# Low-rank forget gates as one 48-row float32r product, and block-diagonal state reads in four 32-column tiles

## The chip, the cores and the metric

The kernel runs on one core of a Trainium2 chip. The metric is the device time of one execution in microseconds (us). Five engines share the work: PE (matmul, with its weight loads shown apart as PEld), DVE (elementwise and reductions), ACT (activations and copies), POOL (elementwise, memset) and SP, whose queue issues every DMA of this kernel.

## What is computed

One layer of a hybrid trunk runs over 2048 prompt tokens, 16 meta tokens and 8 samples of 16 tokens each (D_MODEL 1024). All its inputs are one projection of the normalised rows `h`. Two parts of the gated linear attention (GLA, 4 heads, keys of 128, values of 256) matter here:

```python
log_f = log_sigmoid(g_low @ gla_w2 + gla_gate_b) / GLA_TAU      # g_low: [t, 16], gla_w2: [16, 512]
# per token: S_t = diag(exp(log_f_t)) S_{t-1} + k_t^T v_t ; o_t = q_t S_t
o = einsum('bhid,bhde->bhie', qc * exp(b), s) + einsum('bhij,bhje->bhie', a, vc)
```

The prompt starts from a zero state. Each of the 8 samples starts from a state of its own, `state_gla[b, h]` (128 x 256), so the term `(q exp b) s` takes another `s` for every 16 of the 128 sample rows. The second branch (an indexer that selects 256 keys per query, then attention over them) is not touched.

## The kernel before

`phase1` normalises and transposes the rows, projects them with all columns of the weights, and writes the results to DRAM scratch. `phase_keys` opens it: it goes through the 18 row tiles (meta, 16 of the prompt, the samples), makes the transposed `h` of each (`prep_x`) and the columns needed first (`keys`): attention keys and values, the indexer's key and the 16 gate columns `g_low`. `keys` is a generator in two parts, and the second part of one tile is issued after the first part of the next (`KLAG = 1`). In its second part it transposes the indexer's key and `g_low` into one PSUM tile `ps`, splits the key into high and low halves (`kih` on ACT, `kil` on DVE), copies the 16 gate rows to a small tile `gl` on ACT (L353) and stores them to the scratch `d["gl"]` [16, 2192] by SP (L354). The small tiles of `keys` (`xi`, `xd`, `gl`) share four buffers, tag `evs`. Three projection groups follow (`project`), and in their shadow DVE runs the selection. Projections are written as three float32r products each (`mm3`, L264 to L266): high x high, high x low, low x high.

`phase2` runs attention (`attend`) as the main stream, and beside it a list of side work: `gla_gates`, then `attend_sample`, `gla_sample`, and the 16 prompt chunks of GLA. The first 13 items of it are issued at a priority 1500 earlier than the main stream, so `gla_gates` begins while the last group of `project` is still on PE.

`gla_gates` takes the 2192 columns in five chunks (four of 512 and one of 144). It loads `gl` [16, n] from the scratch (L658), multiplies it for each of 4 heads with `w2` [16, 512] in float32 (L666), which appears as two matmul records per product, and forms the log sigmoid from Abs, Exp and Ln on ACT, a min on DVE and a subtraction on POOL. `w2` is loaded straight from the input (L957) in `gla_pools`, when phase 2 is set up.

`gla_sample` reads the sample states. For each head it loads two tiles `s0` of four states each, clears a tile `qx` [128, 8, 128] on POOL (L923), scatters the queries of sample `b` to columns 16b to 16b+15 of `qx[:, b, :]` (DVE), and adds up eight float32 products of `qx[:, b, :]` with the state of sample `b` in one PSUM tile `po` (L928), 128 columns wide each of which 112 are zero. One product `a` x `v` follows (L929), then the update of the eight states (L935).

The program is built with an ordering pass: instructions are put in order on each engine by priority and by a simulated timeline. So the order in which an engine meets its instructions is fixed in the program, and a change of one operation can move others.

Of the kernel before, what the change touches and what calls it, by code (L numbers as in the profile page):

```python
# [10 lines left out]
F32 = mybir.dt.float32  # L11
F32R = mybir.dt.float32r
# [5 lines left out]
OP = mybir.AluOpType  # L18
# [3 lines left out]
P = 128  # L22
# [6 lines left out]
NB = 8  # L29
# [89 lines left out]
class Trunk:  # L119
# [73 lines left out]
    def scratch(self, ctx):  # L193
        dr = ctx.enter_context(self.tc.tile_pool(name="dr", bufs=1, space=DRAM))
        d = {}
        for n, s, t in (
            ("gq", [512, TT], F32), ("gk", [512, TT], F32), ("gl", [16, TT], F32), ("lf", [512, TT], F32),
            ("gv", [TT, 1024], F32), ("gr", [TT, 1024], F32),
            ("q", [2048, TT], F32R),
            ("ih", [512, TT], F32R), ("il", [512, TT], F32R),  # L200
            ("kd", [P, 4, TT], F32R), ("v", [TT, 256], F32), ("z", [TT, 1024], F32),
            ("ma", [1024, TT], F32), ("mb", [1024, TT], F32),
            ("oa", [1024, TT], F32), ("ob", [1024, TT], F32), ("ya", [1024, TT], F32), ("h", [TT, 1024], F32),
        ):
            d[n] = dr.tile(s, t, name="d_" + n)
        d["mask"] = {j: dr.tile([P, nkeys(j)], BF16, name=f"d_mask{j}") for j in range(16)}
        d["mask"]["s"] = dr.tile([P, SKEY], BF16, name="d_masks")
        d["xt"] = [dr.tile([P, KT, n], F32, name=f"d_xt{q}") for q, n in enumerate(PCN)]
        self.d = d
# [102 lines left out]
    def keys(self, t, x, c, w1, w2):  # L312
# [36 lines left out]
        nc.tensor.transpose(ps[:16, 1, :r], xi[:r, 64:80], self.ident[:r, :r])  # L349
        kc = NKEY if t == "s" else (0 if t == "m" else META + t * P)  # L350
        self.split(self.kih[:, kc : kc + r], self.kil[:, kc : kc + r], ps[:, 0, :r])
        gl = self.ev.tile([16, P], F32, name="gl", tag="evs", bufs=4)
        nc.scalar.copy(gl[:, :r], ps[:16, 1, :r])  # L353
        nc.sync.dma_start(d["gl"][:, c0 : c0 + r], gl[:, :r])  # L354

    def phase_keys(self):

# [294 lines left out]
    def gla_gates(self):  # L652

        nc = self.nc
        for c in range(0, TT, 512):
            n = min(512, TT - c)
            gl = self.gt.tile([16, 512], F32, name="gl", tag="x")
            nc.sync.dma_start(gl[:, :n], self.d["gl"][:, c : c + n])  # L658
            xs, es = [], []
            for g in range(2):  # L660
                x = self.sb.tile([P, 2, 512], F32, name="gx", tag="s4", bufs=SKB)
                e = self.sb.tile([P, 2, 512], F32, name="ge", tag="s4", bufs=SKB)
                for u in range(2):
                    h = 2 * g + u
                    ps = self.pg.tile([P, 512], F32, name="pg")
                    nc.tensor.matmul(ps[:, :n], self.w2[:, h * P : (h + 1) * P], gl[:, :n], start=True, stop=True)  # L666
                    self.act(e[:, u, :n], ps[:, :n], AF.Abs, bias=self.gb[:, h : h + 1])
                    self.ts(x[:, u, :n], ps[:, :n], self.gb[:, h : h + 1], OP.add, 0.0, OP.min)
                self.act(e[:, :, :n], e[:, :, :n], AF.Exp, scale=-1.0)
                xs.append(x)  # L670
                es.append(e)
            for g in range(2):
                x, e = xs[g][:, :, :n], es[g][:, :, :n]
                self.act(e, e, AF.Ln, bias=1.0)
                self.tt(x, x, e, OP.subtract, eng=nc.gpsimd)
                nc.sync.dma_start(self.d["lf"][2 * g * P : (2 * g + 2) * P, c : c + n].rearrange("(h p) t -> p h t", p=P), x)
            yield
# [214 lines left out]
    def gla_sample(self):  # L892
# [20 lines left out]
        for half in range(2):  # L913
            po = self.pg.tile([P, 2, 256], F32, name="pg")
            for u in range(2):
                h = 2 * half + u
                s0 = []
                for w in range(2):
                    t = self.sb.tile([P, 4, 256], F32, name="s0", tag="s4", bufs=SKB)
                    nc.sync.dma_start(t[:], self.i["state_gla"][0, 4 * w : 4 * w + 4, h].rearrange("b k v -> k b v"))  # L920
                    s0.append(t)
                qx = self.sb.tile([P, NB, P], F32, name="qx", tag="s4", bufs=SKB)
                nc.gpsimd.memset(qx[:], 0.0)  # L923
                dg = qx[:].rearrange("p b (c s) -> p (b c) s", s=NS)[:, :: NB + 1, :]
                self.tt(dg.rearrange("p (n u) (w s) -> p n u w s", u=2, w=2), qt[:, h, :, 0:4, :].rearrange("p n (u w) s -> p n u w s", w=2),
                        f[1][0][:, NB * h : NB * h + NB].rearrange("p (n u) w -> p n u w", u=2)[:, :, :, :, None].to_broadcast([P, 4, 2, 2, 8]), OP.mult)
                for bb in range(NB):
                    nc.tensor.matmul(po[:, u, :], qx[:, bb, :], s0[bb // 4][:, bb % 4, :], start=bb == 0, stop=False)  # L928
                nc.tensor.matmul(po[:, u, :], a[:, h, :], v[:, h, :], start=False, stop=True)  # L929
                for bp in range(4):  # L930
                    bs = slice(2 * bp, 2 * bp + 2)
                    vx = self.gm.tile([P, 2, 256], F32, name="vx", tag="m")
# [16 lines left out]
    def gla_pools(self, c):  # L949
# [3 lines left out]
        self.gm = c.enter_context(tc.tile_pool(name="gm", bufs=2))  # L953
        self.pg = c.enter_context(tc.tile_pool(name="pg", bufs=PGB, space=PSUM))
        gc = c.enter_context(tc.tile_pool(name="gc", bufs=1))
        self.w2 = gc.tile([16, 512], F32, name="w2")
        nc.sync.dma_start(self.w2[:], i["gla_w2"][0])  # L957
        self.gb = gc.tile([P, 4], F32, name="gb")
        nc.sync.dma_start(self.gb[:], i["gla_gate_b"][0].rearrange("(h p) -> p h", p=P))
        self.lm = gc.tile([P, 864], U8, name="lm")  # L960
        with tc.tile_pool(name="lf", bufs=1) as lf:
            t = lf.tile([P, 864], F32, name="lmf")
            nc.sync.dma_start(t[:], i["c_levels"])
            nc.vector.tensor_copy(self.lm[:], t[:])
        return gc


# [503 lines left out]
```

## Time and profile before

| | us |
|---|---|
| median of 3 runs | 3657.09 |
| lowest and highest | 3652.93, 3662.06 |
| the profiled execution, its own time | 3653.39 |
| its span, first to last instruction | 3651.6 |
| mean granted TensorE clock | 0.985 of full speed |

Busy time is the time in which an engine executes; an engine that is not busy waits for a semaphore, or has nothing to do. The columns of the windows view are busy us of each engine with the number of its instructions, then the granted clock, the DMA engines' busy share and GB/s. In the views by line, a group's row ends with the idle time of the engine ahead of the group and what ended it. A float32 matmul stands in the trace as two records, a float32r one as one. Records of PE overlap: the distance from start to start is the pace, not the duration of one.

### The profile page before, as it was taken

How to read it: one execution, taken by the hardware profiler on the slowest of the kernel's cores; microseconds unless marked ns; L12 is line 12 of the kernel's file. 1: busy time of each engine (PE TensorE's matmuls, PEld its weight loads, DVE VectorE, ACT ScalarE, POOL GpSimd, SP SyncE). 2: the span in 40 equal slices, each digit the busy share in tenths (PEclk: the TensorE clock that was granted, in tenths of full speed). 3: DMA queues.
4: the chain of work that ended last, by engine and by line, in shares of the span. 5: the costliest groups of instructions: out<-in, count | busy, mean ns of one | idle time of the engine just before them, and what ended most of it. 6: DMA issues, size and time to landing. Idle time of an engine off the chain costs nothing.

```text
span 3651.6 us, 65899 instructions
## 1 busy us (share of the span) xinstructions
PE 3516.6 (96%) x24196; PEld 3224.6 (88%) x24196; DVE 2568.0 (70%) x5971; ACT 1451.5 (40%) x3084; POOL 1048.6 (29%) x1220
## 2 busy tenths in 40 slices
PE   7999999999999999999989999999999999989999
PEld 7999999999999999998976778777778888879998
DVE  7748997799999988943246877777765666555444
ACT  4444223433334234325434555555665443431110
POOL 3122343242343344344301433334410000012221
PEclk9999999999999999999999999999999999999999
DMA  8642443263442345363653333233343345564432
GB/s 266 196 127 84 136 124 96 84 180 106 122 127 75 117 136 166 115 173 122 160 170 106 84 92 85 80 92 85 85 116 89 94 106 138 150 193 140 121 114 62
DMA packets 535810, 448.78 MB, mean 123 GB/s; under 512 B 94032, under 2 KB 507856, under 8 KB 535488
## 3 DMA queue, kind: packets, MB, share of 16 engines
q1 hardware_dynamic: 535488, 444.58, 42.4%
q8 instruction: 190, 3.11, 0.4%
q14 instruction: 132, 1.08, 0.1%
HBM read 288.01 MB, written 156.44 MB: 122 GB/s over the span
## 4 chain that ended last, share of the span: by engine, by line
PE 75%; DVE 13%; DMA 5%; ACT 2%; issue 2%; POOL 1%; SPq 1%; POOLq 0%; DVEq 0%; ACTq 0%
PE pp L266 12%; PE pp L264 12%; PE pp L265 12%; PE oo L1070 6%; PE px L1046 4%; PE pd L264 3%; PE pd L266 3%; PE pd L265 3%; PE pl L1110 2%; PE pl L1111 2%; PE fo L264 2%; PE fo L265 2%; PE fo L266 2%; DVE junk L149 1%; DVE sc L152 1%
## 5 line engine op out<-in xcount | busy, mean ns | idle before, releaser
L149 DVE TENSOR_SCALAR_CACHE_REDUCE junk<-sc,cand 128x272 bf16<-128x272 f32 (+6 forms) x512 | 701.7, 1371 | 17.0
L143 POOL TENSOR_TENSOR wlo<-raw,whi 128x512 fp32r<-128x512 f32 x360 | 487.9, 1376 | 768.0 <-ACT whi L158 704.3
L266 PE MATMUL pp<-whi,xl 128*128 128x256 f32 (+3 forms) x1952 | 560.4, 288 | 4.4 <-DVE xl L143 4.4
L264 PE MATMUL pp<-whi,xh 128*128 128x256 f32 (+3 forms) x1952 | 561.7, 288 | 3.1 <-ACT whi L158 2.1
L264 PE MATMUL pp<-xh,whi 128*128 128x384 f32 (+2 forms) x1728 | 563.0, 326 | 1.4 <-ACT whi L158 1.4
L265 PE MATMUL pp<-xl,whi 128*128 128x384 f32 (+2 forms) x1728 | 563.2, 326 | 0.0
L266 PE MATMUL pp<-xh,wlo 128*128 128x384 f32 (+2 forms) x1728 | 562.1, 326 | 0.1
L265 PE MATMUL pp<-wlo,xh 128*128 128x256 f32 (+3 forms) x1952 | 560.9, 288 | 0.0
L266 PEld LDWEIGHTS pp<-whi,xl 128*128 128x128 f32 (+1 forms) x1952 | 370.4, 190 | 14.6 <-DVE xl L143 6.9
L264 PEld LDWEIGHTS pp<-whi,xh 128*128 128x128 f32 (+1 forms) x1952 | 371.4, 190 | 11.2 <-issue 3.0
L265 PEld LDWEIGHTS pp<-wlo,xh 128*128 128x128 f32 (+1 forms) x1952 | 371.4, 190 | 5.4 <-issue 2.3
L1112 DVE CUSTOM_DVE_ANT_0 lgl<-pl,mkl 128x348 f32<-128x348 f32 (+8 forms) x608 | 297.3, 510 | 83.6 <-PE pl L1111 48.0
L1110 PE MATMUL pl<-kd,q 128*128 128x348 f32 (+14 forms) x800 | 308.1, 388 | 32.7 <-DVE mx L1112 23.9
L264 PE MATMUL pd<-xh,wh 128*128 128x242 f32 (+3 forms) x1152 | 327.9, 285 | 8.6 <-ACT wh L1328 3.8
L264 PEld LDWEIGHTS pp<-xh,whi 128*128 128x128 f32 x1728 | 324.4, 188 | 2.7 <-ACT whi L158 2.0
L266 PE MATMUL pd<-xh,wl 128*128 128x242 f32 (+3 forms) x1152 | 324.6, 282 | 0.8 <-POOL wl L143 0.8
L265 PE MATMUL pd<-xl,wh 128*128 128x242 f32 (+3 forms) x1152 | 325.1, 282 | 0.3 <-DVE xl L143 0.3
L266 PEld LDWEIGHTS pp<-xh,wlo 128*128 128x128 f32 x1728 | 324.1, 188 | 1.2 <-POOL wlo L143 0.4
L265 PEld LDWEIGHTS pp<-xl,whi 128*128 128x128 f32 x1728 | 324.4, 188 | 0.7
L158 ACT CAST whi<-raw 128x512 fp32r<-128x512 f32 (+1 forms) x344 | 199.1, 622 | 314.8 <-DMA raw<-in_w_in 201.3
L155 ACT ACTIVATE lgl<-lgl,mx 128x1040 f32<-128x1040 f32 (+7 forms) x256 | 249.8, 976 | 181.5 <-DVE mx L1114 177.6
L1118 POOL COPY pmeta<-lgl 128x48 f32<-128x48 f32 x256 | 58.7, 229 | 771.4 <-ACT lgl L155 765.0
(250 smaller groups left out, 7842.7 us busy)
## 6 DMA issues: line engine op xcount, KB each, us to landing
raw<-in_w_in SPq DMA_DIRECT2D x360, 256.0 KB, 3.2
q<-d_q SPq DMA_DIRECT2D x272, 128.0 KB, 3.0
d_h<-x SPq DMA_DIRECT2D x17, 512.0 KB, 3.4
d_gv<-en SPq DMA_DIRECT2D x68, 128.0 KB, 2.1
d_gr<-en SPq DMA_DIRECT2D x68, 128.0 KB, 1.8
d_z<-en SPq DMA_DIRECT2D x68, 128.0 KB, 1.7
gr<-d_gr SPq DMA_DIRECT2D x17, 512.0 KB, 3.6
v<-d_gv SPq DMA_DIRECT2D x17, 512.0 KB, 3.9
```

The costliest lines, as they stand in the source:

```text
L143: (eng or self.nc.vector).tensor_tensor(out, a, b, op=op)
L149: (eng or self.nc.vector).tensor_scalar(out, a, s1, s2, op0=op0, op1=op1, **kw)
L155: self.nc.scalar.activation(out, a, f, **kw)
L158: (self.nc.vector.tensor_copy if self.spare else self.nc.scalar.copy)(out, src)
L264: mm(ps, ah(k), bh(k), start=k == 0, stop=False)
L265: mm(ps, ah(k), bl(k), start=False, stop=False)
L266: mm(ps, al(k), bh(k), start=False, stop=k == n - 1)
L1046: nc.tensor.transpose(ps[:, 2 * s + u, :], pe[u][a // KLOW][:, a % KLOW : a % KLOW + P], self.ident[:])
L1070: self.nc.tensor.matmul(oo[0][64 * o : 64 * o + 64, k : k + 2, :], self.v[:, s0 + s, d : d + 64], t[:, 2 * s : 2 * s + 2], start=self.fres ...
L1110: nc.tensor.matmul(ps[:, :m], q[:, u, :], kd, start=True, stop=False)
L1111: nc.tensor.matmul(ps[:, :m], q[:, 2 + u, :], kd, start=False, stop=True)
L1112: nc.vector.tensor_tensor_reduce(lg[z1][:, a : a + m], ps[:, :m], mk[z1][:, a : a + m], 1.0, NEG, OP.add, OP.max, mx[:, s : s + 1])
```

## The change

The low-rank product is made from three float32r parts stacked along the contraction. `keys` now splits the transposed gate rows into a high and a low half (ACT copy, DVE subtraction) and stores both, so the scratch has 32 rows. `gla_gates` loads a tile of 48 rows, high, low and high again (two DMAs), and multiplies it once per head with `w2`, whose 48 rows are high, high and low. `w2` is now loaded three times into a float32 tile, rounded by ACT, and its last 16 rows are made by a DVE subtraction.

In `gla_sample` the tile `qx` shrinks to [128, 4, 4, 16]: samples 2n and 2n+1 fill the 32 columns that go to output rows 32n to 32n+31, and a product of sample 2n+w has 32 columns and writes only those rows of `po`. Products with different n stand next to each other in the program.

```diff
-            ("gl", [16, TT], F32)
+            ("gl", [32, TT], F32R)
...
-        gl = self.ev.tile([16, P], F32, name="gl", tag="evs", bufs=4)
-        nc.scalar.copy(gl[:, :r], ps[:16, 1, :r])
-        nc.sync.dma_start(d["gl"][:, c0 : c0 + r], gl[:, :r])
+        gl = [self.ev.tile([16, P], F32R, name="gl" + x, tag="evs", bufs=4) for x in "hl"]
+        self.split(gl[0][:, :r], gl[1][:, :r], ps[:16, 1, :r])
+        for u in range(2):
+            self.move(d["gl"][16 * u : 16 * u + 16, c0 : c0 + r], gl[u][:, :r])
...
-            gl = self.gt.tile([16, 512], F32, name="gl", tag="x")
-            nc.sync.dma_start(gl[:, :n], self.d["gl"][:, c : c + n])
+            gl = self.gt.tile([48, 512], F32R, name="gl", tag="x")
+            self.move(gl[0:32, :n], self.d["gl"][:, c : c + n])
+            self.move(gl[32:48, :n], self.d["gl"][0:16, c : c + n])
...
-                qx = self.sb.tile([P, NB, P], F32, name="qx", tag="s4", bufs=SKB)
+                qx = self.sb.tile([P, 4, 4, NS], F32, name="qx", tag="s4", bufs=SKB)
                 nc.gpsimd.memset(qx[:], 0.0)
...
-                for bb in range(NB):
-                    nc.tensor.matmul(po[:, u, :], qx[:, bb, :], s0[bb // 4][:, bb % 4, :], start=bb == 0, stop=False)
-                nc.tensor.matmul(po[:, u, :], a[:, h, :], v[:, h, :], start=False, stop=True)
+                for w in range(2):
+                    for n in range(4):
+                        bb = 2 * n + w
+                        nc.tensor.matmul(po[32 * n : 32 * n + 32, u, :], qx[:, n, 2 * w : 2 * w + 2, :], s0[bb // 4][:, bb % 4, :],
+                                         start=w == 0, stop=False, skip_group_check=True)
+                nc.tensor.matmul(po[:, u, :], a[:, h, :], v[:, h, :], start=False, stop=True, skip_group_check=True)
...
-        self.w2 = gc.tile([16, 512], F32, name="w2")
-        nc.sync.dma_start(self.w2[:], i["gla_w2"][0])
+        self.w2 = gc.tile([48, 512], F32R, name="w2")
...
+            t = lf.tile([48, 512], F32, name="w2f")
+            for k in range(3):
+                nc.sync.dma_start(t[16 * k : 16 * k + 16], i["gla_w2"][0])
+            nc.scalar.copy(self.w2[:], t[:])
+            self.tt(self.w2[32:48], t[32:48], self.w2[32:48].bitcast(F32), OP.subtract)
```

## Rows read from the trace of the kernel before

**Rows 1.** The page: busy time, and the chain that ended last by engine.

```profile
PE 3516.6 (96%) x24196; PEld 3224.6 (88%) x24196; DVE 2568.0 (70%) x5971; ACT 1451.5 (40%) x3084; POOL 1048.6 (29%) x1220
...
PE 75%; DVE 13%; DMA 5%; ACT 2%; issue 2%; POOL 1%; SPq 1%; POOLq 0%; DVEq 0%; ACTq 0%
```

**Rows 2.** Windows view of five stages: window and length, then busy us by engine.

```profile
35.00:135.00 100.00, 91.17 (x653) 87.32 (x652) 80.94 (x173) 49.10 (x148) 31.50 (x30) 0.98 0.87 266
135.00:200.00 65.00, 65.00 (x460) 64.76 (x460) 32.98 (x85) 23.29 (x75) 10.03 (x12) 1.00 0.42 130
...
1677.00:1741.00 64.00, 64.00 (x406) 47.65 (x405) 24.88 (x44) 55.70 (x61) 35.07 (x21) 1.00 0.43 136
...
1857.00:1909.00 52.00, 41.46 (x217) 33.13 (x215) 30.58 (x113) 26.49 (x59) 2.65 (x8) 0.84 0.61 169
1909.00:2011.00 102.00, 97.04 (x586) 69.03 (x585) 69.67 (x208) 42.86 (x82) 15.19 (x27) 1.00 0.37 108
```

**Rows 3.** View by line of 1677 to 1741: projections, gate products, their readers on ACT.

```profile
L266 PE MATMUL pp<-whi,xl 128*128 128x256 f32 (+1 forms) x122 | 34.9, 286 | 0.0
...
L666 PE MATMUL pg<-gl,w 16*128 16x512 f32 (+1 forms) x40 | 19.4, 573 | 0.0
...
L155 ACT ACTIVATE ge<-pg,gb 128x512 f32<-128x512 f32 (+1 forms) x20 | 12.2, 621 | 51.6 <-PE pg L666 51.5
```

**Rows 4.** PE's timeline: around a gate product, around L1173, and 512-column float32r products.

```profile
1682.19 0.28 PE L265 MATMUL pp<-wlo,xh 128*128 128x256 f32 x1
1682.40 1.12 PE L666 MATMUL pg<-gl,w 16*128 16x512 f32 x2
1683.45 0.39 PE L266 MATMUL pp<-whi,xl 128*128 128x256 f32 x1
1683.68 0.28 PE L264 MATMUL pp<-whi,xh 128*128 128x256 f32 x1
1683.79 0.28 PE L265 MATMUL pp<-wlo,xh 128*128 128x256 f32 x1
...
1745.98 0.29 PE L1173 MATMUL pg<-ks,qsl 128*128 128x272 f32 x1
1746.11 0.28 PE L264 MATMUL pp<-whi,xh 128*128 128x256 f32 x1
...
3302.32 0.40 PE L264 MATMUL fo<-woh,mgh 128*128 128x512 f32 x1
3302.56 0.40 PE L265 MATMUL fo<-wol,mgh 128*128 128x512 f32 x1
```

**Rows 5.** The chain in order of time: two of four runs of L928, one of L1070.

```profile
1933.45 3.46 PE pg L928 x16
...
1954.48 3.72 PE pg L928 x16
...
1960.37 3.60 PE oo L1070 x32
```

**Rows 6.** PE's timeline inside a run of L1070, which writes 64 rows per product.

```profile
1960.78 0.38 PE L1070 MATMUL oo<-pt,v 128*64 128x256 f32 x1
1960.78 0.38 PE L1070 MATMUL oo<-st,v 128*64 128x256 f32 x1
1960.99 0.38 PE L1070 MATMUL oo<-pt,v 128*64 128x256 f32 x1
```

**Rows 7.** The line of the memset in `gla_sample`: count, ns min/median/max.

```profile
L923 POOL MEMSET qx<- x4: 952/953/957, 1901.8 to 1995.7; 128x1024 f32 x4
```

**Rows 8.** `keys` in 35 to 135: DVE by line, a wait, landing times of L354.

```profile
L143 DVE TENSOR_TENSOR kil<-pk,kih 128x128 fp32r<-128x128 f32 (+1 forms) x10 | 2.8, 280 | 2.1 <-ACT kih L158 1.9
...
ACT gl L353 <- DVE kil L143: 6.9, 5, 1.9
...
DMA to landing us min/median/max: 1.3/3.2/6.1
```

**Rows 9.** Timeline of SP and ACT ahead of the gates: start us, length us, instruction.

```profile
1622.24 0.59 SPq L957 DMA_DIRECT2D w<-in_gla_w  x1
...
1678.50 0.69 ACT L155 ACTIVATE ge<-pg,gb 128x512 f32<-128x512 f32 x1 [45.90 <-PE pg L666]
```

More of the change, by code (lines that the diff above doesn't have):

```diff
@@ L196, in scratch @@
         for n, s, t in (
-            ("gq", [512, TT], F32), ("gk", [512, TT], F32), ("gl", [16, TT], F32), ("lf", [512, TT], F32),
+            ("gq", [512, TT], F32), ("gk", [512, TT], F32), ("gl", [32, TT], F32R), ("lf", [512, TT], F32),
             ("gv", [TT, 1024], F32), ("gr", [TT, 1024], F32),
@@ L921, in gla_sample @@
                     s0.append(t)
-                qx = self.sb.tile([P, NB, P], F32, name="qx", tag="s4", bufs=SKB)
+                qx = self.sb.tile([P, 4, 4, NS], F32, name="qx", tag="s4", bufs=SKB)
                 nc.gpsimd.memset(qx[:], 0.0)
-                dg = qx[:].rearrange("p b (c s) -> p (b c) s", s=NS)[:, :: NB + 1, :]
-                self.tt(dg.rearrange("p (n u) (w s) -> p n u w s", u=2, w=2), qt[:, h, :, 0:4, :].rearrange("p n (u w) s -> p n u w s", w=2),
+                self.tt(qx[:, :, ::3, :].rearrange("p n u (w s) -> p n u w s", w=2), qt[:, h, :, 0:4, :].rearrange("p n (u w) s -> p n u w s", w=2),
                         f[1][0][:, NB * h : NB * h + NB].rearrange("p (n u) w -> p n u w", u=2)[:, :, :, :, None].to_broadcast([P, 4, 2, 2, 8]), OP.mult)
-                for bb in range(NB):
-                    nc.tensor.matmul(po[:, u, :], qx[:, bb, :], s0[bb // 4][:, bb % 4, :], start=bb == 0, stop=False)
-                nc.tensor.matmul(po[:, u, :], a[:, h, :], v[:, h, :], start=False, stop=True)
+                for w in range(2):
[4 more added lines that the diff above has]
+                nc.tensor.matmul(po[:, u, :], a[:, h, :], v[:, h, :], start=False, stop=True, skip_group_check=True)
                 for bp in range(4):
```

## Prediction

> **What bounds the kernel now.** I began with the page: PE is busy for 96% of the span and holds 75% of the chain that ended last, DVE only 13% [rows 1]. So the question for each edit is how much PE time it takes away, and whether PE is the limit in that place. The windows view answers the second part. From 1677 to 1741, where the gate products run, PE is busy for all 64.00 us, ACT for 55.70. From 1909 to 2011, where the sample states are read, PE is busy for 97.04 of 102. The place where rows are added, `keys`, is different: from 35 to 135 PE has 8.8 us of idle time, DVE is busy for 80.94 of 100 and the DMA engines for 0.87; from 135 on PE is full again [rows 2]. So PE time saved in the two later places should shorten the kernel, and a delay in the first can lengthen it. The view by line and PE's timeline then give the prices.
>
> **The gate products.** In the 64 us there are three groups of projection matmuls of 122 records each [rows 3], of which the row of L266 stands for the two of L264 and L265. They follow each other at 0.11 to 0.12 us: a float32r record of 256 columns starts 0.11 us after the one before [rows 4], and I use 0.118. That is 366 x 0.118 = 43.2 us, so the 40 records of L666 took the other 20.8, although their busy sum is 19.4 [rows 3]. One product seen alone agrees: from the projection at 1682.19 to the second projection after the pair, at 1683.68, are 1.49 us, where two steps would have been 0.24, so a pair costs 1.25, and 16 x 1.25 plus four short ones makes about 21 [rows 4]. After the change there are 20 single float32r records, 16 of 512 columns and 4 of 144. A 512-column float32r record takes 0.24 from start to start [rows 4], so they stream for 16 x 0.24 + 4 x 0.07 = 4.1 us (the 0.07 scaled by columns). What the trace does not show is a float32r product of 48 rows among products of 128. The lower bound of its switching is nothing: L1173, float32r of 128 rows, is followed by a projection at its own pace, 0.13 for 272 columns [rows 4]. The upper bound is that of the 16-row float32 pair, 1.25 less two float32 records of 512 columns; a float32 record of 256 columns takes 3.46/16 = 0.216 [rows 5], so two of 512 take 0.86 and the switching 0.39. It is nearer to L1173 in type and nearer to the pair in rows; I take 0.15. So 4.1 + 20 x 0.15 = 7.1 us, and the gates save 20.8 - 7.1 = **13.7 us** of PE (8.9 to 16.7 by the bounds).
>
> All of it is filled by projections, which are the next work of PE there. But the gates' own chain does not shorten as much: ACT is busy for 55.70 of the 64 us, so at most 8.3 can go. [...]
>
> **The sample queries.** The four runs of L928 are 3.46 and 3.72 us, twice each within 0.01 [rows 5], 14.4 together: 64 records at 0.22. After the change they are again 64 records, each of 32 columns of weights, and the saving hangs on how many run at once. The nearest thing is L1070, which writes 64 of the 128 output rows: its two halves start at the same hundredth of a microsecond, and the next pair comes 0.21 later [rows 6]. So two column tiles share a slot of 0.21; a run of 32 records takes 3.60, which is 16 slots and 0.2 for getting in and out [rows 5]. If four tiles share a slot, a head takes 4 slots, 0.85 + 0.2, and say 0.1 for the third and fourth tile: 1.15, four heads 4.6. Saved: 14.4 - 4.6 = 9.8. With two at once it is 8 slots, 1.9 a head, 6.8 saved; with none, 0.8 lost to the switching. I take four, because the two tiles of L1070 show no trace of a shared resource (a start 0.00 us apart), and the program puts four different tiles side by side. PE is the limit for 95% of this stage, so **9.3 us** are gained. [...]
>
> The memset shrinks to a quarter of its elements, from 0.953 us [rows 7]. POOL is busy for 15 of these 102 us, but PE waits for `qx` behind it now and then; between 0 and 4 x 0.95, near the bottom since most of it is covered by attention's matmuls: **0.5 us**.
>
> **What is added in `keys`.** Each of 18 tiles gets one DVE subtraction of 16x128 from PSUM and one more DMA. The nearest DVE row is `kil`, the same 128 columns, 0.28 us [rows 8]. Ten of the tiles fall in the stage where DVE, not PE, sets the pace: 10 x 0.25 = 2.5 us. The subtraction needs ACT's copy of the high half, which itself waits for `kil` (five times, 6.9 us) [rows 8], so in the worst place DVE waits another 0.3 each, 5.5 in all; in the best the idle of DVE (19 of 100 us) takes it and it costs nothing. SP's extra issue is covered by SP's own gaps, and what is queued behind it are stores. There is one more wait: `gl` takes two of the four `evs` buffers, so the next tile's `xi` or `xd` may have to wait until a store has landed, 3.2 us at the median [rows 8]. Most of it passes while the tile is in its other steps; 0.5 us in all. Together **3.0 us** lost (0 to 8).
>
> **What is moved.** `w2` gets two more DMAs, an ACT cast and a DVE subtraction. They stand before the first gate product at 1677. ACT is idle for 45.90 us ahead of that and `w2` was only loaded at 1622 [rows 9], so some 50 us cover them; without that cover they would be about 2 us once. The second DMA of each `gl` chunk delays a side chain that has projections to cover it: nothing.
>
> **The sum.** -13.7 + 2.7 - 9.3 - 0.5 + 3.0 = -17.8 us. On the profiled execution (span 3651.6, its own time 3653.39) that is 3635.6. The median of the runs is 3.7 above the profiled one, so I forecast **3639.3 us**. About 0.3%, 11 us, is what a measurement can tell from no change.
>
> **The rivals.**
> The **two-tile** case: only two of four column tiles share a slot. For it, the trace shows only two; against it, there is no sign of a limit at two. It costs 3 us: 3642. [...] Chance 0.10, and 0.07 more that tiles of 32 share nothing: 14.4 + 0.8 spent, total -13.7 + 2.7 + 0.8 - 0.5 + 3.0 = -7.7, 3649.
> **ACT sets the gates' pace**: the saved PE time comes back entirely behind 1857. For it, ACT's 55.70 of 64; against it, PE has other work all the time and idles only a fifth after 1857. -9.3 - 0.5 + 3.0 = -6.8: 3650. Chance 0.13.
> **The good bounds**: the 48-row product switches as freely as L1173, nothing is given back at 1857, and the idle of DVE takes what `keys` gets: -16.7 - 9.3 - 0.5 = -26.5, 3631. Chance 0.13.
> **The buffers of `keys`** (the other side): if each of the ten tiles waits for a landing on DVE, 3.2 us each, 32 us are lost against the 20.8 gained: +11, 3668. It decides from 2.1 us a tile. Against it: ten tiles in 100 us are 10 us each, and a store lands 3.2 after its issue. Chance 0.07, a landing nearer to the 6.1 of the slowest included.
> The forecast itself has 0.50. The order that the ordering pass makes anew can shift each case by several us; I hold its own range at 3631 to 3646.
>
> **Numbers.** Faster: 0.50 + 0.10 + 0.13, less 0.02 for the upper edge of the forecast: 0.71. Same: 0.07 + 0.13, that edge, and 0.01 of the buffers' case: 0.23. Slower: the other 0.06. The range reaches from the good bounds with some of the new order's scatter, 3627, to just above the two cases near 3650: 3653.
>
> **What would show it.** Right: L666 with 20 records and under 8 us of PE; four L928 records starting together, 16 in about 1.1 us; PE still full to the end of the projections, which come some 13 us earlier, with the idle time behind them about 13 us instead of 10.5; the stage up to 135 longer by 3. Wrong: records of L928 at 0.11 or 0.22 apart; PE idle between gate products; DVE waits on a DMA at `xd` or `xi`; or a new order in attention whose idle time outweighs the rest.

## The result, and the profile after

The changed kernel runs at a median of 3626.29 us (3623.17 to 3628.36, 4 runs), the kernel before at 3657.32 beside it. The ratio is 0.9914, with a 95% interval of 0.9897 to 0.9931: 31 us faster, where 17.8 were forecast. It ends 13 us below the forecast and 0.7 below the low end of the range. That 0.7 is less than the medians of the kernel before differ between its sets of runs (3653.35 to 3657.32); the 13 is more. The profiled execution has a span of 3625.2 us, 26.4 less than that of before; the other 4.6 us are how the two profiled executions lie to their medians (3653.39 to 3657.32, 3626.96 to 3626.29).

The page, its busy line and the engines' shares of the chain that ended last [rows 1]:

```profile
PE 3488.2 (96%) x24176; PEld 3211.3 (89%) x24176; DVE 2565.4 (71%) x5990; ACT 1452.7 (40%) x3085; POOL 1044.9 (29%) x1220
...
PE 67%; DVE 17%; DMA 7%; issue 3%; ACT 3%; POOL 2%; SPq 1%; POOLq 0%; DVEq 0%; ACTq 0%
```

PE's busy time fell by 28.4 us and is still 96% of the span. DVE's share of the chain rose from 13 to 17%. The windows [rows 2]; the last three begin later than those of before, because the work in them does:

```profile
35.00:135.00 100.00, 87.39 (x582) 83.75 (x581) 71.13 (x160) 46.15 (x136) 29.65 (x28) 0.92 0.81 240
135.00:200.00 65.00, 62.79 (x459) 62.05 (x458) 42.54 (x111) 23.16 (x79) 9.80 (x12) 0.99 0.53 161
1700.00:1764.00 64.00, 64.00 (x471) 55.81 (x472) 25.50 (x51) 58.54 (x67) 36.09 (x22) 1.00 0.52 158
1868.00:1920.00 52.00, 43.75 (x263) 34.09 (x264) 29.61 (x104) 24.46 (x52) 1.54 (x5) 0.90 0.57 163
1920.00:2022.00 102.00, 96.40 (x654) 68.63 (x650) 76.93 (x244) 55.53 (x107) 13.96 (x31) 0.98 0.38 110
```

The `keys` stage has become poorer: in the 100 us from 35 on, PE executes 582 matmuls instead of 653, and DVE, which I had expected to be busier, is busy for 71.13 us instead of 80.94. PE's granted clock is 0.92 of full speed there instead of 0.98. The gate stretch is as full as before. Behind the projections PE idles for 8.25 of 52 us, not for more than the 10.54 of before.

Where the time went is seen best from the first and last start of four lines: the transpose of the gate columns in `keys` (L349), the gate products, the projections, and the first product of the main attention's logits. Before:

```profile
L349 PE MATMUL pk<-ident,xi x18: 171/272/273, 45.6 to 187.4; 128*16 128x128 f32 x17, 16*16 16x16 f32 x1
...
L666 PE MATMUL pg<-gl,w x40: 281/587/692, 1677.3 to 1736.8; 16*128 16x512 f32 x32, 16*128 16x144 f32 x8
...
L266 PE MATMUL pp<-xh,wlo x1728: 276/334/423, 180.4 to 1857.5; 128*128 128x384 f32 x159, 128*128 128x256 f32 x30, 128*128 128x272 f32 x3
...
L1110 PE MATMUL pl<-kd,q x800: 221/398/798, 1869.8 to 3223.0; 128*128 128x348 f32 x96, 128*128 128x344 f32 x16, 128*128 128x456 f32 x7, 128*128 128x328 f32 x7
```

And after:

```profile
L349 PE MATMUL pk<-ident,xi x18: 171/272/273, 46.4 to 201.4; 128*16 128x128 f32 x17, 16*16 16x16 f32 x1
...
L669 PE MATMUL pg<-gl,w x20: 330/492/502, 1699.9 to 1754.7; 48*128 48x512 f32 x16, 48*128 48x144 f32 x4
...
L266 PE MATMUL pp<-xh,wlo x1728: 276/334/582, 192.5 to 1867.6; 128*128 128x384 f32 x159, 128*128 128x256 f32 x30, 128*128 128x272 f32 x3
...
L1120 PE MATMUL pl<-kd,q x800: 219/394/747, 1873.8 to 3197.2; 128*128 128x348 f32 x96, 128*128 128x344 f32 x16, 128*128 128x456 f32 x7, 128*128 128x328 f32 x7
```

The differences of these times cut the span into pieces that add up to it:

| us | before | after | change |
|---|---|---|---|
| to the end of `keys` (last L349) | 187.4 | 201.4 | +14.0 |
| from there to the first gate product | 1489.9 | 1498.5 | +8.6 |
| first gate product to the last projection | 180.2 | 167.7 | -12.5 |
| last projection to the first logits | 12.3 | 6.2 | -6.1 |
| first to last logits (main attention) | 1353.2 | 1323.4 | -29.8 |
| the rest | 428.6 | 428.0 | -0.6 |

The gate products saved less than I expected, and less than their stretch. One of them among projections, after:

```profile
1704.87 0.28 PE L266 MATMUL pp<-whi,xl 128*128 128x256 f32 x1
1705.07 0.49 PE L669 MATMUL pg<-gl,w 48*128 48x512 f32 x1
1705.49 0.38 PE L264 MATMUL pp<-whi,xh 128*128 128x256 f32 x1
1705.71 0.28 PE L265 MATMUL pp<-wlo,xh 128*128 128x256 f32 x1
```

From 1704.87 to 1705.71 are 0.84 us, where two steps of projections would have been 0.24, so this product costs 0.60. Counted over all of them, from the projection ahead of the first to the third matmul behind the last: before, 60.25 us hold 331 projections at 0.1171, which leaves 21.5 for the 40 records; after, 55.65 hold 379 at 0.1174, which leaves 11.2 for the 20. So 10.3 of the 12.5 us are the gate products. The other 2.2 are 17 matmuls of the samples' attention that the new order no longer puts into this stretch (PE executes 1226 matmuls in it before and 1189 after; 20 of the 37 fewer are the gates').

`keys` lost far more than forecast, and attention won far more than the queries in it. The queries themselves stand in the chain in order of time [rows 5], one head of four:

```profile
1955.40 1.00 PE pg L933 x16
```

It was 3.46 and 3.72 for a head, so four heads went from 14.4 to 4.0. Almost 20 us of the gain in attention have nothing to do with them.

### The profile page after: what moved, and what is told of

Its sections match the earlier page's. It is cut to its first block, busy times and chain, and to the rows that moved or that the text cites. A ratio compares the mean times of both kernels' runs of the same rounds, so it can differ in the third digit from the quotient of the medians.

```text
span 3625.2 us, 65962 instructions
## 1 busy us (share of the span) xinstructions
PE 3488.2 (96%) x24176; PEld 3211.3 (89%) x24176; DVE 2565.4 (71%) x5990; ACT 1452.7 (40%) x3085; POOL 1044.9 (29%) x1220
## 4 chain that ended last, share of the span: by engine, by line
PE 67%; DVE 17%; DMA 7%; issue 3%; ACT 3%; POOL 2%; SPq 1%; POOLq 0%; DVEq 0%; ACTq 0%
PE pp L266 10%; PE pp L264 10%; PE pp L265 10%; PE oo L1080 6%; DVE junk L149 4%; PE px L1056 4%; PE pd L264 3%; PE pd L266 3%; PE pd L265 3%; PE pl L1120 2%; PE pl L1121 2%; DVE lgl L1122 2%; PE fo L264 2%; PE fo L265 2%; PE fo L266 2%
## 5 line engine op out<-in xcount | busy, mean ns | idle before, releaser
L266 PEld LDWEIGHTS pp<-whi,xl 128*128 128x128 f32 (+1 forms) x1952 | 372.5, 191 | 17.5 <-DVE xl L143 13.7
L1120 PE MATMUL pl<-kd,q 128*128 128x348 f32 (+14 forms) x800 | 304.6, 384 | 21.1 <-DVE mx L1122 11.8
```

The source lines that it names most:

```text
L266: mm(ps, al(k), bh(k), start=False, stop=k == n - 1)
L1120: nc.tensor.matmul(ps[:, :m], q[:, u, :], kd, start=True, stop=False)
```

## Experiments

The same pieces of every run, from the same four rows of its own trace, in us (medians stand at the experiments). Each row is one profiled execution, which can lie off its kernel's median: 10.5, 8.9 and 7.1 us below it in e4_onebuf, e9_pool and e3_store, 6.7 above it in e11_onebuf.

| | end of `keys` | to first gate | gate to last proj. | to logits | attention |
|---|---|---|---|---|---|
| before | 187.4 | 1489.9 | 180.2 | 12.3 | 1353.2 |
| after | 201.4 | 1498.5 | 167.7 | 6.2 | 1323.4 |
| e1_queries | 186.6 | 1491.1 | 180.2 | 12.3 | 1340.1 |
| e2_gates | 201.3 | 1496.1 | 167.7 | 6.0 | 1344.0 |
| e3_store | 195.2 | 1493.9 | 180.2 | 12.4 | 1349.7 |
| e4_onebuf | 185.8 | 1492.3 | 168.1 | 6.0 | 1316.0 |
| e5_adjacent | 199.4 | 1494.6 | 167.7 | 6.9 | 1324.3 |
| e6_late | 189.0 | 1492.3 | 168.1 | 6.0 | 1319.2 |
| e6_lategates | 187.8 | 1494.6 | 167.6 | 6.0 | 1327.7 |
| e7_twice | 198.5 | 1491.8 | 175.6 | 5.4 | 1348.5 |
| e8_bufs3 | 197.2 | 1492.5 | 181.7 | 12.6 | 1348.8 |
| e9_pool | 185.7 | 1488.0 | 181.6 | 12.7 | 1326.1 |
| e10_onebufpool | 189.3 | 1493.5 | 167.7 | 6.0 | 1307.5 |
| e11_onebuf | 190.1 | 1497.6 | 167.7 | 6.0 | 1320.7 |

My theory after the result had three parts: the PE time that each edit removes counts where it is removed; the loss in `keys` comes from the shared buffers rather than from the subtraction; and the rest of the gain in attention comes from the new order of instructions. The rival was that work alone sets all pieces.

### One part at a time

**e1_queries**: before, with only the query part of the diff.

> Before, with the change to the sample queries alone (qx of 32 columns, four column tiles). Its instruction order is that of before up to the end of the gate chunks and new from there on. Theory A, the work alone counts: the query products lose 10 us of PE and nothing else moves; 3657 - 10 = 3647, and the main attention's other products keep their pace. Theory B, the new order that this edit brings is what made attention 26 us shorter beyond the queries: 3657 - 10 - 26 = 3621, with the waits of PE for the softmax maximum near 10 us instead of 22. Theory C, the new order is luck that each edit draws afresh: anything from 3620 to 3670, attention shorter or longer by up to 25 us than by the queries alone.

3642.19 us, ratio 0.9966 (0.9955 to 0.9977): 13.4 faster. Only attention moved, by 13.1. That is theory A with a few us more; theory B is out. Theory C, which allowed anything from 3620 to 3670, this run can't rule out.

**e2_gates**: the changed kernel with the queries of before.

> The change without its query part: gates in one float32r product, sample queries as before. Up to the end of the gate chunks its instruction order is that of the changed kernel. Theory A, the work alone counts: keys about 13 us later, projections another 5, the gates 8 to 14 of PE back, attention as before; about 3657 + 18 - 8 = 3667, slower than before. Theory B, the query edit brings the better order: the same 3667. Rival: the better order of attention comes with the gates' edit, then 3626 + 10 = 3636. Theory C (each edit draws its own order): 3640 to 3685.

3648.33 us, ratio 0.9985 (0.9976 to 0.9994): 7.3 faster, against 3667 by work alone. `keys` loses 13.9, the gate stretch wins 12.5, the way to the first logits 6.3, and attention 9.2 although no operation in it changed. The two parts alone give 13.4 + 7.3 = 20.7 us, together 31: they don't add up, so something else than their work counts.

**e3_store**: before, splitting and storing both halves of the gate rows and nothing more; the gate product reads the high half alone.

```diff
-        gl = self.ev.tile([16, P], F32, name="gl", tag="evs", bufs=4)
+        gl = [self.ev.tile([16, P], F32R, name="gl" + x, tag="evs", bufs=4) for x in "hl"]
...
-            nc.sync.dma_start(gl[:, :n], self.d["gl"][:, c : c + n])
+            nc.sync.dma_start(gl[:, :n], self.d["gl"][0:16, c : c + n].bitcast(F32))
```

> Before, with nothing of the change but the storing of both halves in the keys stage (the subtraction and the second transfer). The gate product stays float32 with 16 rows and reads the high half alone, so the gates are computed from rounded rows. If the loss of 13 us in the keys stage is due to what is added there, the first index product comes 12 to 14 us later than before, as in the changed kernel, and the projections 18 later; if it needs the other edits, it comes 0 to 3 later. The time: 3657 + 13 to 18 by work alone, 3670 to 3675; by a new order in attention up to 25 us either side of that.

3669.59 us, ratio 1.0039 (1.0024 to 1.0054): 14 slower, 9 in the profiled execution. `keys` ends 7.8 later. PE's order behind the gate products is that of before, instruction for instruction, and so the gate stretch is 180.2 again and attention 1349.7, within 3.5. This run gives an idea of the scatter of a piece whose order doesn't change, and shows that the loss in `keys` needs neither the new product nor the queries.

### What `keys` lost

**e4_onebuf** and, the same kernel timed again, **e11_onebuf**: both halves in one buffer, so `keys` takes as many small buffers as before. Subtraction and both transfers stay.

```diff
-        gl = [self.ev.tile([16, P], F32R, name="gl" + x, tag="evs", bufs=4) for x in "hl"]
-        self.split(gl[0][:, :r], gl[1][:, :r], ps[:16, 1, :r])
+        gl = self.ev.tile([48, P], F32R, name="gl", tag="evs", bufs=4)
+        self.split(gl[0:16, :r], gl[32:48, :r], ps[:16, 1, :r])
...
```

> The changed kernel with both gate halves of a tile in one buffer (rows 0 to 15 and 32 to 47 of one tile), so the four small buffers of the keys stage are used as in before; subtraction and both transfers stay. If the buffers hold the stage up, its loss falls from 10.7 to 12.7 us at the first index product to 3 or less, and the kernel runs at 3626 - 8 to 10 = 3617. If the subtraction, the second transfer and the order they bring are the cause, the loss stays at 10 or more and so does 3626.

> The changed kernel with one buffer for both gate halves once more, for its time beside the three others: 3600 to 3616 as in its first runs, keys as before, first gate product within 3 of 1678.

3610.3 us, ratio 0.9878 (0.9858 to 0.9899), and 3605.98, ratio 0.9866 (0.9849 to 0.9884). `keys` ends at 185.8 and 190.1, against 187.4 before and 201.4 after: the loss is gone, though every added operation is still there.

**e8_bufs3**: before, with the four buffers cut to three and no operation added (the same edit at `xi` and `xd`).

```diff
-        gl = self.ev.tile([16, P], F32, name="gl", tag="evs", bufs=4)
+        gl = self.ev.tile([16, P], F32, name="gl", tag="evs", bufs=3)
```

> Before, with the four small buffers of the keys stage (tag evs) cut to three, and nothing else. No operation and no transfer is added. If a shortage of these buffers is what the changed kernel lost in keys, the last transposes of keys come 8 to 14 us later than before, the first gate product 10 to 20, and the time is 3654 + 10 to 20 = 3664 to 3674. If the subtraction and the second transfer were the cause, nothing moves in keys, and the time is that of before within what its order in attention (16 of 100 places differ) brings.

3666.55 us, ratio 1.0037 (1.0025 to 1.0048). `keys` ends at 197.2, 9.8 late. Together the two settle it: the shortage of buffers costs 8 to 14 us, the subtraction and the second transfer nothing that can be seen. How it costs stands in DVE's waits from 35 to 150 (what waited for what, us in total, times, longest). Before:

```profile
DVE st L180 <- DMA x<-in_x_prompt: 10.6, 7, 2.6
...
DVE st L180 <- ACT xi L327: 1.4, 1, 1.4
```

The changed kernel:

```profile
DVE st L180 <- DMA x<-in_x_prompt: 17.7, 10, 2.8
DVE st L180 <- ACT xi L327: 8.6, 5, 2.2
```

e8_bufs3, three buffers and nothing added:

```profile
DVE st L180 <- DMA x<-in_x_prompt: 16.8, 10, 2.8
DVE st L180 <- ACT xi L327: 9.8, 6, 2.3
```

e4_onebuf, everything added and the buffers as before:

```profile
DVE st L180 <- DMA x<-in_x_prompt: 8.4, 8, 1.9
...
DVE st L180 <- ACT xi L327: 1.1, 1, 1.1
```

No line of them says "buffer". DVE waits in its statistics for `xi`, which lives in one of these buffers, and for the next rows `x`. In the changed program the load of `x` often stands further back in SP's queue, behind the store of a finished tile's keys, and the order on all engines in `keys` is another one. So the shortage acts through the order that was made with it: what waits is two steps away from it. PE's order up to the first gate product differs from that of before in 383 of 11116 matmuls in e3_store and in 352 in e8_bufs3. That it is the order, and not a wait for a buffer on the chip, was argued from these rows only. The cost itself is of two kinds. Up to the end of `keys` PE is idle for 23.5 us before, and for 29.4, 30.8 and 32.2 in the changed kernel, e3_store and e8_bufs3. And in the changed kernel the granted clock is at 0.5 of full speed for 20.5 us of this piece, against 6.8 in the other three; half of the difference is 6.9 us of the 14.0, the idle time another 5.9.

### What attention won

**e7_twice**: the changed kernel, with every gate product issued twice.

```diff
                     nc.tensor.matmul(ps[:, :n], self.w2[:, h * P : (h + 1) * P], gl[:, :n], start=True, stop=True)
+                    nc.tensor.matmul(ps[:, :n], self.w2[:, h * P : (h + 1) * P], gl[:, :n], start=True, stop=True)
```

> The changed kernel with each of the 20 gate products issued twice, the second writing the same rows again. It adds 20 records of a 48-row float32r product: by my price (0.26 each of the 16 long ones) 5 us between the first gate product and the last projection, 167.6 to about 172.5, by the price of the bounds 4 to 10. By work alone the kernel ends 5 us later, 3631. But its order in attention differs from that of the changed kernel in three places of four: if the order carries the 16 to 20 us by which attention is shorter beyond the queries, attention comes anywhere from 1323 to 1343 and the time from 3631 to 3650.

3648.01 us, ratio to before 0.9983 (0.9974 to 0.9992): 5.3 faster than before, where the changed kernel is 31. The gate stretch takes 175.6, 7.9 longer. Of these the 40 products take 16.5 us, counted as above, where the 20 took 11.2: 5.3 for the added ones, 0.27 each, as expected. Most of them stand right behind their first, so this is not the price of one among projections. The rest is 1.1 us of PE idle time and matmuls of the samples' attention that this order puts back into the stretch. Attention is 25 us longer, 1348.5 instead of 1323.4, although the edit touches nothing in it. Nearly the same work, another order, 25 us.

**e6_late** and **e6_lategates**: `keys` as before; the gate rows are loaded three times and split in `gla_gates` (now high, high and low, so that the low part of `w2` is made in rows 16 to 31). The second has the queries of before.

```diff
+            gf = self.gt.tile([48, 512], F32, name="gf", tag="b")
+            for k in range(3):
+                nc.sync.dma_start(gf[16 * k : 16 * k + 16, :n], self.d["gl"][:, c : c + n])
...
+            nc.scalar.copy(gl[:, :n], gf[:, :n])
+            self.tt(gl[32:48, :n], gf[32:48, :n], gl[32:48, :n].bitcast(F32), OP.subtract)
...
```

> The changed kernel with the split moved out of keys: the rows are stored as in before, loaded three times per chunk of gla_gates, rounded there by ACT and split by DVE. The gate products and the sample queries are those of the changed kernel; the order in keys is that of before. First index product and first gate product within 3 us of before (1677). From the first gate product to the last projection 167.6 us if the gate product alone sets that stretch, up to 5 more if ACT, which gets five more casts, does. If work alone set the attention (first to last logits 1323 in the changed kernel), the whole kernel comes out 17 to 22 us below the changed one, about 3606. If the order does, the attention is drawn anew: 1323 to 1353 less 10, so 3606 to 3636.

> The same with the sample queries of before. By work alone the attention takes 1344, as in the gates-only kernel, and the time is 3648 - 20 = 3628. By order it can be 1330 to 1360: 3614 to 3644. The difference to the run with the new queries says what the queries are worth under a third order: 10 by work.

3605.22 us, ratio 0.987 (0.9855 to 0.9884), and 3615.1, ratio 0.9896 (0.9879 to 0.9912). The late split costs nothing in the gate stretch (168.1), so ACT doesn't set its pace. Under this third order the queries are worth 9.9 us in the medians and attention is as short as in the changed kernel. The gates' edit alone brings 38 us here and 7.3 in e2_gates; the difference is `keys` (13.5 us) and the order in attention (1327.7 against 1344.0).

What a good order has and a bad one lacks is seen first in PE's waits in attention. The greatest is for DVE, which takes the maximum of a logits tile (`mx`) and so frees its PSUM buffer, one of three. Before, from the first to the last logits:

```profile
PE pl L1110 <- DVE mx L1112: 23.9, 23, 2.8
```

After:

```profile
PE pl L1120 <- DVE mx L1122: 11.8, 15, 2.7
```

And in e7_twice:

```profile
PE pl L1121 <- DVE mx L1123: 23.1, 22, 2.8
```

It is 23.8, 25.7 and 22.4 in e1_queries, e3_store and e8_bufs3, and 18.1 in e2_gates; in the short ones (e4, e5, both e6, e11) 11.7 to 14.0. One such wait of before in the timelines of DVE, POOL and PE:

```profile
2290.78 1.36 DVE L143 TENSOR_TENSOR f<-b 128x256 f32<-128x256 f32 x5
2292.05 0.38 DVE L761 COPY_PREDICATED a<-lm,pg 128x192 f32<-128x192 uint8 x1
2292.31 2.67 DVE L143 TENSOR_TENSOR f<-b 128x64 f32<-128x64 f32 x7
...
2295.45 0.51 DVE L1112 CUSTOM_DVE_ANT_0 lgl<-pl,mkl 128x348 f32<-128x348 f32 x1
...
2292.35 1.06 POOL L143 TENSOR_TENSOR m<-k,x 128x256 f32<-128x256 f32 x1 [1.56 <-issue]
2293.38 1.59 POOL L143 TENSOR_TENSOR mq<-q,x 128x256 f32<-128x256 f32 x2
...
2296.02 0.66 PE L1110 MATMUL pl<-kd,q 128*128 128x348 f32 x1 [2.62 <-DVE mx L1112]
```

The twelve subtractions of `gla_factors` (tile `f`) stand together ahead of the logits tile `lgl`. The last seven are smaller than the first five but take 2.67 us, 0.38 each, exactly while POOL works on the `m` and `mq` of the same chunk. PE stands still for 2.62. The same twelve after the change, and POOL around them:

```profile
2290.89 2.09 DVE L143 TENSOR_TENSOR f<-b 128x256 f32<-128x256 f32 x12 [1.16 <-POOL mq L143]
...
2289.81 1.05 POOL L143 TENSOR_TENSOR mq<-mq,f 128x512 f32<-128x512 f32 x1
2293.81 0.87 POOL L143 TENSOR_TENSOR m<-k,x 128x256 f32<-128x256 f32 x1 [2.95 <-issue]
```

They begin when POOL has ended one chunk and are done before it begins the next: 2.09 us for all. The view by line, from 1900 to 2700, before:

```profile
L143 DVE TENSOR_TENSOR f<-b 128x128 f32<-128x128 f32 (+4 forms) x198 | 55.5, 348 | 2.0 <-POOL mq L143 1.9
```

And after:

```profile
L143 DVE TENSOR_TENSOR f<-b 128x128 f32<-128x128 f32 (+4 forms) x198 | 41.2, 278 | 4.7 <-POOL mq L143 4.5
```

The mean is 332 to 352 ns in the five kernels with a long attention (before, e1, e3, e7, e8), 327 in e2_gates, and 277 to 283 in the short ones.

PE's waits are only a part of it; the other is its granted clock. In these traces the clock has two values, full and half (1.0 and 0.5 in the clock records of before and after). A transpose of 128 columns (`px`) follows the one before it at 0.109 us at full clock and at 0.213 at half, so where PE is the limit a microsecond at half clock loses half a microsecond. At the end of the wait of 2.62 us shown above the clock falls to half, and in all a long attention stands at half clock for longer than a short one. The windows of that moment before, then of attention before, after and in e7_twice:

```profile
2295.50:2298.90 3.40, 2.88 (x11) 2.77 (x12) 3.22 (x16) 1.03 (x2) 1.08 (x2) 0.50 0.31 77
1869.80:3223.00 1353.20, 1288.85 (x9196) 1075.06 (x9197) 927.62 (x3224) 690.19 (x1486) 320.69 (x600) 0.98 0.38 102
...
1873.80:3197.20 1323.40, 1267.87 (x9220) 1061.40 (x9219) 918.26 (x3242) 691.89 (x1493) 316.04 (x600) 0.99 0.39 106
...
1871.30:3219.80 1348.50, 1284.29 (x9214) 1071.05 (x9215) 927.96 (x3229) 691.85 (x1492) 317.57 (x600) 0.98 0.38 104
```

By the traces' clock records attention stands at half clock for 53.7 us before, 33.4 after and 64.8 in e7_twice, and PE is idle in it for 64.3, 55.5 and 64.2. Between e7_twice and the changed kernel that is 8.7 us of idle time and 15.7 of clock (half of 31.4), 24.4 of the 25.1. Between e2_gates and e6_lategates it is 3.3 and 13.7, where attention differs by 16.3. The same count over the whole span, for every run (PE's idle time, time at half clock, and the span less the one and half of the other):

| us | PE idle | at half clock | what is left |
|---|---|---|---|
| before | 135.0 | 110.2 | 3461.5 |
| after | 137.0 | 96.6 | 3439.9 |
| e1_queries | 140.2 | 96.7 | 3449.7 |
| e2_gates | 143.7 | 100.7 | 3450.4 |
| e3_store | 151.3 | 94.1 | 3462.3 |
| e4_onebuf | 124.0 | 71.8 | 3438.2 |
| e5_adjacent | 132.9 | 90.8 | 3439.9 |
| e6_late | 127.0 | 69.2 | 3441.1 |
| e6_lategates | 126.5 | 61.2 | 3453.2 |
| e7_twice | 142.5 | 120.7 | 3444.8 |
| e8_bufs3 | 151.0 | 95.6 | 3462.1 |
| e9_pool | 130.9 | 68.7 | 3456.3 |
| e10_onebufpool | 124.2 | 68.6 | 3432.5 |
| e11_onebuf | 129.0 | 83.6 | 3440.2 |

What is left behaves as work does: the queries alone take 11.8 off, the gates alone 11.1, both together 21.6, the doubled product adds 4.9, and where splits, stores or buffers alone differ it moves by 3 or less. Only the two POOL runs take off 5.2 and 7.7 that are not explained. That the two edits don't add up in time is nearly all in the first two columns. An order acts by how long PE waits, and by how much of the time its clock is low; that the waits bring the low clock was seen at many of them, not shown by an experiment.

**e9_pool**: before, with these subtractions on POOL. **e10_onebufpool**: e4_onebuf with the same.

```diff
-        e = self.nc.vector
...
-                self.tt(t.rearrange("p (h n c) -> p h n c", h=4, n=n), x, y, OP.subtract, eng=e)
+                self.tt(t.rearrange("p (h n c) -> p h n c", h=4, n=n), x, y, OP.subtract, eng=self.nc.gpsimd)
```

> Before, with the twelve subtractions of gla_factors (tile f) on POOL instead of DVE; nothing else. If attention is long because these subtractions stand together in DVE's order ahead of the evictions that free PE's logits buffers, PE's wait for the maximum falls from 23.9 us to 12 or less and attention from 1353 to 1330 to 1342, the time to 3630 to 3643, though the edit touches neither gates nor queries. If the block of subtractions is not the cause, the wait stays above 20 and the time within 5 of before.

> The changed kernel with one buffer for both gate halves and with the twelve subtractions of gla_factors on POOL. Its order already keeps the subtractions apart, and PE waits 12.0 us for the maximum. If only the blocks cost, it gains 0 to 6 us; if every subtraction on DVE costs PE something, 10 or more. If POOL is late with the factors, it loses up to 10.

e9_pool: 3632.27 us, ratio 0.9939 (0.9924 to 0.9954), 21.7 faster than before without any of the change. Attention is 1326.1, shorter by 27.1, more than I expected; the wait for the maximum fell only to 16.6, less than I expected, so the wait that bears that name is not all that the subtractions cost. In attention PE is idle for 6.8 us less, and the time at half clock falls from 53.7 to 26.0, which is worth 13.9; the remaining 6.4 are not explained. Part of the effect may again be order, since this edit shifts the order of attention too. e10_onebufpool: 3595.09 us, ratio 0.984 (0.9825 to 0.9855), the fastest of all: 58.9 below before, and 10.9 below e11_onebuf beside it. Attention is 1307.5, 13.2 shorter than in e11_onebuf. That even a good order still paid for the subtractions on DVE fits this, but the order changed with them here too.

### The column tiles

**e5_adjacent**: the changed kernel, the two products of one column tile next to each other.

```diff
-                for w in range(2):
-                    for n in range(4):
+                for n in range(4):
+                    for w in range(2):
```

> The changed kernel with the eight query products of a head issued in the order of their samples, so that two that write the same 32 rows stand next to each other. Every other instruction stands as in the changed kernel. If four column tiles share a slot when their products are next to each other, the two of one tile must now follow each other: 5 slots instead of 2 per head at about 0.22, so 4 heads are some 2.6 us longer, 3629, and the records of L933 go from 62 ns each to about 0.14. If tiles share nothing and a 32-column product is just short, nothing changes: 62 ns and 3626. The attention keeps its shorter time either way, since the order is the same: the 26 us beyond the queries stay if the order made them.

3624.21 us, ratio to before 0.9917 (0.9902 to 0.9932), as the changed kernel. The chain again, one head:

```profile
1949.86 1.02 PE pg L933 x16
```

The 5 slots that I expected did not come. The records of a head show why: in both kernels the sixteen records (eight products of two) start in four groups of four, the groups 0.22 to 0.24 us apart and the four of a group 0.01. So it looks as if each tile works through its own row of products, and their order among tiles counts for nothing here. Nor is a 32-column product just quick: from group to group it keeps the pace that 128 columns had, 0.22 us.

## Why the prediction was right and wrong

**The bound.** Right: PE is busy for 96% still, and PE time removed in a PE-bound place came out of the span, 10.3 and 10.4 us.

**The gate products.** Right in mechanism, with the switching of one product mis-sized: 13.7 us forecast, 10.3 measured, inside the bounds of 8.9 to 16.7 but near the low one. A 48-row product of 512 columns costs about 0.61 among projections and one of 144 columns 0.46; less 0.24 and 0.07 of streaming, the switching is 0.37 to 0.39, not my 0.15 but the 0.39 of the 16-row pair. So it went with the few rows, as far as these three kinds of product tell, and not with the type. The sign "under 8 us of PE" failed with it: the 20 products take 11.2. ACT as the pace, the rival at 3650, did not happen: projections filled the time, and the first to the last gate product went from 59.5 only to 54.8.

**The hand-over.** Wrong in sign: the sum has +2.7 us for it, a term that no run shows; in its place the runs showed 6.1 us won, 6.2 instead of 12.3. All kernels with the new product have 5.4 to 6.9 from the last projection to the first logits, all with the old one 12.3 to 12.7. The +2.7 was an estimate that took the side work to be the same list, standing further back. But PE's order decides what is done ahead of the first logits, and it was drawn anew. The windows of this piece, before and after:

```profile
1857.50:1869.80 12.30, 7.83 (x34) 5.37 (x32) 5.32 (x21) 3.77 (x10) 0.00 (x0) 0.68 0.77 243
...
1867.60:1873.80 6.20, 4.58 (x27) 3.46 (x26) 2.44 (x5) 1.91 (x4) 0.00 (x0) 0.95 0.77 264
```

PE is idle in it for 1.6 us instead of 4.5, and its clock is at half for 0.7 us instead of 7.8; 2.9 and half of 7.1 are about the 6.1. PE's waits there, before:

```profile
PE pg L1185 <- ACT slg L155: 2.0, 1, 2.0
PE pg L1173 <- DVE ks L143: 1.2, 2, 0.6
PE pg L1197 <- ACT pn L1192: 0.7, 1, 0.7
PE pl L1110 <- issue: 0.6, 1, 0.6
```

And after:

```profile
PE pg L1183 <- DVE ks L143: 0.8, 1, 0.8
PE pg L1215 <- DVE on L143: 0.8, 1, 0.8
```

Before, more of the samples' attention (L1173 to L1199) stood there, each step waiting for another engine. That the order alone did this was only argued.

**The queries.** Right: 9.8 forecast before the factor for the stage, 10.4 measured in the chain (1.00 us a head where 1.15 was forecast), and 9.9 between the two late-split kernels. Four tiles share a slot: in the changed kernel the records of four tiles start within 0.02 us of each other and the next four 0.22 to 0.24 us later. The two-tile rival and the one where none share are out. The memset went from 0.953 to 0.312 us; PE waited for `qx` once before, 0.5 us, and not at all after, which is the size of that term, too small for a piece of the span to show.

**`keys`.** The step that failed first: "together 3.0 us lost (0 to 8)", of which 2.5 for the subtraction and 0.5 for the buffers. 14.0 were lost, and it is the other way round. The subtraction and the second transfer cost nothing visible (e4_onebuf), the buffers 8 to 14 (e3_store, e8_bufs3, e2_gates and the changed kernel). My rival of the buffers had the place right, but looked for DVE waiting for a landing, priced at 3.2 a tile; the traces show a shifted order instead, at about 1 us a tile. I divided by the time a tile takes and did not count how many buffers one tile holds: three of four before, four of four after, with two tiles under way.

**The order.** The step that took the result out of the range: "the order that the ordering pass makes anew can shift each case by several us", with nothing for it in the sum. It shifted attention by 25 us for nearly the same work (e7_twice against the changed kernel), and by 16 between two orders of the same gates and old queries (e2_gates, e6_lategates). The 26.4 us between the two traces are thus 10.3 from the gate products, 10.4 from the queries, 2.2 of other work moved out of the gate stretch, 6.1 at the hand-over, 19.4 in attention beyond the queries and 0.6 at the end, less 14.0 lost in `keys` and 8.6 behind it. Of my own terms, gates and queries came to 20.7, where 23.0 were forecast; the rest of the sum was wrong. Of the 19.4, 8.8 are PE's idle time (the wait for the maximum alone fell by 12.1, others grew) and about 10.2 the granted clock, half of the 20.3 us less at half clock. The clock in attention was the term put at nothing.

What was won outside the gates and the queries, 28.3 us, and what was lost in `keys` and behind it, 22.6, nearly cancel. Over the whole span PE is idle for 2.0 us more than before, not less, and 6.8 are won by the clock. That the total stayed near the work of the two edits was luck.

**Left open.** The 8.6 us between the end of `keys` and the first gate product: 7.9 of them are PE's idle time (22.4 before, 30.3 after). Three kernels whose PE order to that point is that of the changed one lose 6.2, 4.7 and 1.9 there (e2_gates, e5_adjacent, e7_twice), and two executions of one program 2.4 and 7.7 (e4, e11), so much of it may be scatter. Why one order sets the factors beside POOL's work and another between it was seen, not explained.

## What to carry to other kernels

Before costing an added operation, count the buffers that a loop step holds and how many steps are under way: a second small tile in a shared pool cost 8 to 14 us here, its arithmetic and its transfer nothing that could be seen, and one buffer for both gave it all back. Where a pass orders the instructions, any edit is also a new order for everything behind it; run the edit beside a neutral variant that changes the order (here, a doubled product) before crediting the edit with its gain. Set PE's idle time and its time at half clock apart from the work: what is left tells what an edit is worth by itself. And when PE waits for DVE, look at what stands ahead on DVE and at what POOL does in that moment: moving twelve small subtractions to POOL, with the order that came of it, gave 21.7 us before and 10.9 on top of e11_onebuf, where the two parts of the change alone gave 13.4 and 7.3.

## What the runs showed of the hardware that I had not expected

- DVE's small subtractions of two SBUF inputs slow down beside POOL. Counted over the records from 1900 to 2700, before: 53 of the 198 `f` subtractions ran for three tenths of their time or more while POOL was in a two-input operation and took 0.62 us on average, the other 145 took 0.25. After, the numbers are 15 and 183, at the same two means. Shape by shape it is the same before: 0.42 alone and 0.75 beside POOL for 256 elements, 0.26 and 0.65 for 64, 0.17 and 0.58 for 16. On POOL itself they take 345 ns on average (e9_pool), no more than the 348 on DVE.
- Column tiles do not mind the order of their products: sixteen records of four tiles take 1.00 us when the products are spread over the tiles, and 1.02 when those of a tile are adjacent.
- A 48-row float32r product of 512 columns between products of 128 rows costs 0.61 us on average (14 of them in the changed kernel), against 0.24 from start to start for a 128-row one [rows 4]: the step ahead of it is 0.21 instead of 0.12, its own 0.42, the one behind it 0.22. An added one, mostly right behind another, costs 0.27 (e7_twice).
- A wait of PE can cost more than its length. Of the 12 over 1.5 us in attention before, 7 have a stretch at half clock at their end or close behind; of the 9 after, 4; of the 13 in e7_twice, 12.
